# A hybrid decoder layer on one core: attention's products with the values, 40 places later in the scheduler's order of preference

## Chip, cores and metric

The kernel runs on one core of a Trainium2 chip. The metric is the device time of one execution in microseconds, and the number compared is the median of several executions. The kernel is written against a tile framework: the code names the work and the tiles, and a scheduler decides, before anything runs, in which fixed order each engine gets its instructions. On the chip every engine takes its own list in that order and waits on semaphores.

## What is computed

One decoder layer for a sequence of 2048 tokens, width 1024, in float32. The input is scaled and shifted by a conditioning vector; one projection feeds two groups of heads; their outputs are normalised, projected and added; a gated feed-forward network follows. The part that the change touches is group A, stick-breaking attention with 8 heads of 64:

```
z = einsum('bhqd,bhkd->bhqk', q, k) * scale
log_beta = log_sigmoid(z);  log_one_minus = where(causal, log_sigmoid(-z), 0)
tail = cumsum(log_one_minus, axis=3, reverse=True) - log_one_minus
w = where(causal, exp(log_beta + tail), 0)
out = einsum('bhqk,bhkd->bhqd', w, v)
```

Each weight is a sigmoid times the product of (1 - sigmoid) over all keys between it and the query, so a running product goes backwards over the keys. The last line is the product with the values.

## The kernel before

The sequence is cut into four tiles of 512 tokens (`t` = 0 to 3). `attend(t)` works through 8 heads; for each head it goes backwards over the key tiles `jt` = t to 0. One pair (head, key tile) is a step, so there are 8 x (1 + 2 + 3 + 4) = 80 steps. A step has two halves.

- **Four rows of 128 queries.** For each: two matmuls into the PSUM tile `z` (L549, L550), two sigmoids on ScalarE into `pp` and `beta` (L551, L552), on the diagonal two masks on GpSimd (L554, L556), the backward running product on VectorE (L563) and the multiplication of `beta` with it (L565; GpSimd for two rows of the four, VectorE for the others).
- **Four blocks of 128 keys** (`kb`). For each: up to four transposes of the weights on TensorE into the PSUM tile `wt` (L573), a copy `wh` on ScalarE that rounds to the matmul's format (L577), the remainder `wl = wt - wh` on VectorE (L578), and the products with the values, one with `wh` (L579) and one with `wl` (L581), both accumulated in the PSUM tile `o_ps`.

There are two buffers each of `wt`, `wh` and `wl`, and one of `o_ps`. So the transposes of block 2 wait until `wh` and `wl` of block 0 have been read out of `wt`. When a head is done, `o_ps` is copied and added into `ot` (L585, L586) and stored; the next head's first product waits for that.

Between the steps stands other work, "side work" below: `spread` takes from two generators in turn, so that the code order is a mixture. Beside `attend(t)` run the gated linear attention of tile t, the projections of tile t+1 (L293 to L295: 24 matmuls for one column tile; L302 to L304) and the preparation of later weights. Beside the last three heads of the last tile runs the mixer's output stage (L758, L791, L443 and the lines about them); lines L919 to L936 set it up, and stand in the code behind five heads of the last tile.

The scheduler numbers every instruction in the order of the code. Going through a simulated time, it gives each engine, of the instructions whose inputs and buffers it holds for ready, the one with the smallest number. `Urgent(engine, n)` shifts that number by n for the calls that go through it (a negative n makes it larger, so the instruction is less preferred). Before the change `act`, `dve` and `pool` have a positive shift, and `lazy`, with -90, is used for the mixer's output projection. The products of attention have their plain number through `pe`.

Of the kernel before, what the change touches and what calls it, by code (L numbers as in the profile page):

```python
# [60 lines left out]
NS3 = 21  # L61
NS0 = 35
LAZY = 90
PLO = (0,2)
ORD = 1
WP = 5.1
# [20 lines left out]
def layer(tc, x, c, w_ada, b_ada, w_in, gla_w_gate, gla_b_gate, sb_norm_g, gla_norm_g, w_out,  # L87
          ln1_g, ln1_b, w_ff_gate, w_ff_up, conv_w, conv_b, w_down, ln2_g, ln2_b, out):
    nc = tc.nc
# [15 lines left out]
    act, dve, pool = Urgent(nc.scalar), Urgent(nc.vector), Urgent(nc.gpsimd)  # L105
    pe = nc.tensor
    lazy = Urgent(nc.tensor, -LAZY) if LAZY else nc.tensor
    x, out = x[0], out[0]
    w_ada, w_in, w_out = w_ada[0], w_in[0], w_out[0]
    w_ff_gate, w_ff_up, w_down = w_ff_gate[0], w_ff_up[0], w_down[0]  # L110
# [100 lines left out]
    with tc.tile_pool(name="ada", bufs=1, reuse_waits="tile") as ada:  # L211
# [36 lines left out]
        for n in FIRST:  # L248
            ada_cols(KT + done, n, wa_first if done == 0 else None)
            ada_cols(done, n)  # L250
            cs = slice(done * P, (done + n) * P)
# [274 lines left out]
    def attend(t):  # L526
        for h in range(8):
            p, half = h // 2, h % 2
            rs = slice(64 * half, 64 * half + 64)
            q2 = sb.tile([P, 2, TQ], F32R, name="q2")  # L530
            for j in range(2):
                for rep in range(2):
                    nc.sync.dma_start(q2[64 * rep:64 * rep + 64, j, :].bitcast(F32), dq[p][t][j, rs, :])
            o_ps = psm.tile([P, TQ], F32, name="o_ps", bufs=1)
            carry = [None] * NB
            for jt in range(t, -1, -1):
                k2 = sb.tile([P, TQ], F32R, name="k2", bufs=3)
                for j in range(2):
                    nc.sync.dma_start(k2[64 * j:64 * j + 64, :].bitcast(F32), dk[p][jt][j, rs, :])
                v2 = sb.tile([P, NB, P], F32R, name="v2", bufs=3)  # L540
                nc.sync.dma_start(v2.bitcast(F32), dv[h // 4][jt][:, :, h % 4, :])
                ws = []
                for i in range(NB):
                    n = P * (i + 1) if jt == t else TQ
                    beta = sb.tile([P, TQ], F32, name="beta", bufs=NBETA)
                    pp = sb.tile([P, TQ + 1], F32, name="pp", bufs=NPP)
                    z = psm.tile([P, TQ], F32, name="z")
                    qs = slice(i * P, (i + 1) * P)
                    pe.matmul(z[:, 0:n], q2[:, 0, qs], k2[:, 0:n], start=True, stop=False)  # L549
                    pe.matmul(z[:, 0:n], q2[:, 1, qs], k2[:, 0:n], start=False, stop=True)  # L550
                    nc.scalar.activation(pp[:, 0:n], z[:, 0:n], AF.Sigmoid, scale=-1.0)  # L551
                    nc.scalar.activation(beta[:, 0:n], z[:, 0:n], AF.Sigmoid)  # L552
                    if jt == t:
                        nc.gpsimd.affine_select(pp[:, n - P:n], pp[:, n - P:n], pattern=[[-1, P]],  # L554
                                                compare_op=ALU.is_gt, fill=1.0, base=0, channel_multiplier=1)
                        nc.gpsimd.affine_select(beta[:, n - P:n], beta[:, n - P:n], pattern=[[-1, P]],  # L556
                                                compare_op=ALU.is_gt, fill=0.0, base=0, channel_multiplier=1)
                        nc.gpsimd.memset(pp[:, n:n + 1], 1.0)
                        first = 1.0
                    else:  # L560
                        first = carry[i][:, 0:1]
                        nc.gpsimd.tensor_copy(pp[:, TQ:TQ + 1], first)
                    nc.vector.tensor_tensor_scan(pp[:, 0:n][:, ::-1], pp[:, 0:n][:, ::-1],  # L563
                                                 beta[:, 0:n], first, ALU.mult, ALU.bypass)
                    (nc.gpsimd if i in PMU and jt < PMJ else nc.vector).tensor_mul(beta[:, 0:n], beta[:, 0:n], pp[:, 1:n + 1])  # L565
                    carry[i] = pp
                    ws.append(beta)
                for kb in range(NB):
                    q0 = kb if jt == t else 0
                    ks = slice(kb * P, (kb + 1) * P)  # L570
                    wt = psm.tile([P, TQ], F32, name="wt")
                    for i in range(q0, NB):
                        pe.transpose(wt[:, i * P:(i + 1) * P], ws[i][:, ks], ident)  # L573
                    wh = sb.tile([P, TQ], F32R, name="wh")
                    wl = sb.tile([P, TQ], F32R, name="wl")
                    cs = slice(q0 * P, TQ)
                    nc.scalar.copy(wh[:, cs], wt[:, cs])  # L577
                    nc.vector.tensor_sub(wl[:, cs], wt[:, cs], wh[:, cs])  # L578
                    pe.matmul(o_ps[:, cs], v2[:, kb, :], wh[:, cs],  # L579
                                     start=(jt == t and kb == 0), stop=False)  # L580
                    pe.matmul(o_ps[:, cs], v2[:, kb, :], wl[:, cs],  # L581
                                     start=False, stop=(jt == 0 and kb == NB - 1))
                yield WU if jt < t else WD
            ot = sb.tile([64, TQ], F32, name="ot", bufs=1)
            nc.scalar.copy(ot, o_ps[64:P, :])  # L585
            nc.vector.tensor_add(ot, ot, o_ps[0:64, :])  # L586
            nc.sync.dma_start(do[p][t][rs, :], ot)
            yield 0.0
# [190 lines left out]
    def mixer_out(t, ahead=None, n_ahead=1):  # L779
# [7 lines left out]
        for i in range(8):  # L787
# [13 lines left out]
            act.copy(hi, o)  # L801
            (nc.gpsimd if i in PLO else dve).tensor_sub(lo, o, hi)
            oh.append(hi)
# [95 lines left out]
    for t in range(NT - 1):  # L899
        spread(attend(t), 8 * (t + 2), 8 * (WD + t * WU), with_ada(between(t), ada_todo), S0 * (WP * 25 + WC * 8 + WL))  # L900
    last = attend(NT - 1)
    spread(last, LASTN * (NT + 1), LASTN * (WD + (NT - 1) * WU), with_ada(between(NT - 1), ada_todo), S3 * (WP * 13 + WC * 8))
    for f in ada_todo:
# [460 lines left out]
```

## Time and profile before

| | us |
|---|---|
| median of 3 runs | 2909.52 (2899.4 to 2913.5) |
| the profiled execution, its time | 2910.72 |
| the profiled execution, its span | 2909.0 |
| TensorE busy in the span | 2695.8 (93%) |
| VectorE busy in the span | 2092.0 (72%) |
| mean granted TensorE clock | 0.955 of full speed |

The span is from the first to the last instruction; the profiled execution's time is 1.7 us longer. Attention runs from 108 to 1431 us of the span; after it comes the rest of the mixer and the feed-forward network. Busy time of a matmul contains its way through the array, so rows of busy matmuls overlap, and the distance between two starts is what a matmul costs the one behind it.

### The profile page before, as it was taken

The numbers are of one execution on the slowest core, as the hardware profiler recorded it, in microseconds if no ns is written. First come the engines' busy times: TensorE is split into PE (matmuls) and PEld (weight loads), VectorE is DVE, ScalarE is ACT, GpSimd is POOL, SyncE is SP. The second block draws the span as 40 slices with busy tenths as digits, with TensorE's granted clock in tenths as the row PEclk, the third lists the DMA queues.
The fourth block names the chain that finished last, engine by engine and source line by source line (L and its number), as shares of the span: only waits on it lengthen the run. The fifth ranks groups of instructions, "written<-read, shape, count | busy, mean of one in ns | idle before, by whom it ended". The sixth has DMA issues, their size and how long they took to land. (4 is left out here: it accounts for less than half of the span.)

```text
span 2909.0 us, 38667 instructions
## 1 busy us (share of the span) xinstructions
PE 2695.8 (93%) x13123; PEld 2176.0 (75%) x13123; DVE 2092.0 (72%) x2984; ACT 1126.2 (39%) x1955; POOL 1206.8 (41%) x1271
## 2 busy tenths in 40 slices
PE   7989998989999988989779999898999999999998
PEld 6867887777788765567558778786788888788886
DVE  6375568568878878897676867776777777255988
ACT  2443244365656546534322333223322324332331
POOL 2550222155457674454573455754655554100000
PEclk8989999999999999989789999999999999999999
DMA  8977865767589876466795365545633334655564
GB/s 315 362 251 259 273 237 187 249 193 248 185 261 312 295 245 196 140 200 198 272 335 178 114 182 170 176 133 157 182 110 113 105 106 151 194 169 157 175 211 130
DMA packets 438173, 591.04 MB, mean 203 GB/s; under 512 B 28926, under 2 KB 276952, under 8 KB 437976
## 3 DMA queue, kind: packets, MB, share of 16 engines
q1 hardware_dynamic: 436248, 582.28, 61.9%
q0 software_dynamic: 1728, 6.29, 0.6%
q8 instruction: 104, 1.70, 0.2%
q14 instruction: 93, 0.76, 0.1%
HBM read 417.14 MB, written 171.32 MB: 202 GB/s over the span
## 5 line engine op out<-in xcount | busy, mean ns | idle before, releaser
L563 DVE TENSOR_TENSOR_SCAN pp<-pp,beta 128x512 f32<-128x512 f32 (+2 forms) x320 | 401.5, 1269 | 70.5 <-POOL beta L556 41.7
L565 POOL TENSOR_TENSOR beta<-beta,pp 128x512 f32<-128x512 f32 (+2 forms) x160 | 205.3, 1283 | 291.2 <-DVE pp L563 248.7
L1043 PE MATMUL acc<-t,w_lo 128*128 128x512 f32 x640 | 248.0, 395 | 16.4 <-DVE w_lo L102 16.4
L1041 PE MATMUL acc<-t,w_hi 128*128 128x512 f32 x640 | 252.2, 395 | 4.8 <-ACT k L1099 2.5
L1042 PE MATMUL acc<-t,w_hi 128*128 128x512 f32 x640 | 251.2, 393 | 2.1 <-POOL t L102 2.1
L578 DVE TENSOR_TENSOR wl<-wt,wh 128x512 fp32r<-128x512 f32 (+1 forms) x320 | 185.5, 597 | 71.6 <-ACT wh L577 71.2
L577 ACT CAST wh<-wt 128x512 fp32r<-128x512 f32 (+1 forms) x320 | 161.8, 530 | 180.9 <-PE wt L573 172.9
L551 ACT ACTIVATE pp<-z 128x512 f32<-128x512 f32 (+2 forms) x320 | 173.3, 544 | 138.2 <-PE z L550 83.5
L102 POOL TENSOR_TENSOR w_lo<-wsum,w_hi 128x1024 fp32r<-128x1024 f32 x80 | 204.6, 2558 | 30.4 <-ACT w_hi L102 30.4
L102 ACT CAST w_hi<-w_raw 128x512 fp32r<-128x512 f32 (+2 forms) x169 | 121.4, 740 | 247.5 <-PE acc L1042 93.0
L293 PE MATMUL acc<-hh,w_hi 128*128 128x512 f32 x480 | 194.9, 407 | 3.6 <-DVE st L102 3.0
L573 PE MATMUL wt<-ident,beta 128*128 128x128 f32 x1088 | 184.2, 286 | 14.6 <-DVE beta L565 6.3
L294 PE MATMUL acc<-hl,w_hi 128*128 128x512 f32 x480 | 192.6, 402 | 1.4 <-DVE hl L102 1.4
L295 PE MATMUL acc<-hh,w_lo 128*128 128x512 f32 x480 | 191.4, 400 | 0.5 <-POOL w_lo L102 0.5
L552 ACT ACTIVATE beta<-z 128x512 f32<-128x512 f32 (+2 forms) x320 | 171.2, 543 | 22.6 <-PE wt L573 22.6
L581 PE MATMUL o_ps<-wl,v 128*128 128x512 f32 (+1 forms) x320 | 135.0, 426 | 44.9 <-DVE wl L578 42.5
L573 PEld LDWEIGHTS wt<-ident,beta 128*128 128x128 f32 x1088 | 139.9, 147 | 46.2 <-DVE beta L565 8.8
L1043 PEld LDWEIGHTS acc<-t,w_lo 128*128 128x128 f32 x640 | 121.4, 190 | 45.2 <-DVE w_lo L102 19.8
L549 PE MATMUL z<-k,q 128*128 128x512 f32 (+2 forms) x320 | 140.9, 444 | 13.2 <-ACT beta L552 10.7
L102 ACT CAST w_hi<-wsum 128x1024 fp32r<-128x1024 f32 x80 | 84.0, 1050 | 176.9 <-PE wt L1042 72.8
L102 DVE TENSOR_TENSOR wsum<-w_raw 128x512 f32<-128x512 f32 x80 | 102.8, 1288 | 66.5 <-POOL w_lo L102 54.2
L554 POOL TENSOR_SCALAR_AFFINE_SELECT pp<-pp 128x128 f32<-128x128 f32 x128 | 56.0, 438 | 226.7 <-ACT pp L551 223.1
(341 smaller groups left out, 7603.5 us busy)
## 6 DMA issues: line engine op xcount, KB each, us to landing
w_raw<-in_w_ff_gate_dram SPq DMA_DIRECT2D x48, 512.0 KB
w_raw<-in_w_ff_up_dram SPq DMA_DIRECT2D x48, 512.0 KB
k<-dk SPq DMA_DIRECT2D x160, 128.0 KB
v<-dv SPq DMA_DIRECT2D x80, 256.0 KB
da<-cv SPq DMA_DIRECT2D x40, 512.0 KB
dsa<-cv SPq DMA_DIRECT2D x80, 256.0 KB
w_hi<-dwi_0h SPq DMA_DIRECT2D x39, 512.0 KB
w_lo<-dwi_0l SPq DMA_DIRECT2D x39, 512.0 KB
```

The costliest lines, as they stand in the source:

```text
L102: return f(*args, **kw)
L293: nc.tensor.matmul(ps, hi[:, k % 4, cs], xh[k], start=(k == 0), stop=False)
L294: nc.tensor.matmul(ps, hi[:, k % 4, cs], xl[k], start=False, stop=False)
L295: nc.tensor.matmul(ps, lo[:, k % 4, cs], xh[k], start=False, stop=(k == nk - 1))
L551: nc.scalar.activation(pp[:, 0:n], z[:, 0:n], AF.Sigmoid, scale=-1.0)
L563: nc.vector.tensor_tensor_scan(pp[:, 0:n][:, ::-1], pp[:, 0:n][:, ::-1], beta[:, 0:n], first, ALU.mult, ALU.bypass)
L565: (nc.gpsimd if i in PMU and jt < PMJ else nc.vector).tensor_mul(beta[:, 0:n], beta[:, 0:n], pp[:, 1:n + 1])
L573: pe.transpose(wt[:, i * P:(i + 1) * P], ws[i][:, ks], ident)
L578: nc.vector.tensor_sub(wl[:, cs], wt[:, cs], wh[:, cs])
L1041: nc.tensor.matmul(ps, w[0][:, k, :], t[k][:, 0, :], start=first and k == 0, stop=False, **add)
L1042: nc.tensor.matmul(ps, w[0][:, k, :], t[k][:, 1, :], start=False, stop=False, **add)
L1043: nc.tensor.matmul(ps, w[1][:, k, :], t[k][:, 0, :], start=False, stop=k == 3, **add)
```

## The change

The products with the values are issued through a second wrapper, which makes their number larger by 40. Nothing is added or removed: the same instructions, tiles, buffers and DMAs. What may differ is the order in which the scheduler lays down the instructions of each engine, and, by its simulated time, the order on the other engines and queues.

```
+OLATE = 40
...
+    late = Urgent(nc.tensor, -OLATE)
...
-                    pe.matmul(o_ps[:, cs], v2[:, kb, :], wh[:, cs],
+                    late.matmul(o_ps[:, cs], v2[:, kb, :], wh[:, cs],
                                      start=(jt == t and kb == 0), stop=False)
-                    pe.matmul(o_ps[:, cs], v2[:, kb, :], wl[:, cs],
+                    late.matmul(o_ps[:, cs], v2[:, kb, :], wl[:, cs],
                                      start=False, stop=(jt == 0 and kb == NB - 1))
```

## Rows read from the trace of the kernel before

**Rows 1.** Stretches: length, busy us (instructions) of each engine, TensorE clock, DMA share, GB/s.
```profile
100.00:400.00 300.00, 280.11 (x1674) 240.16 (x1674) 177.64 (x302) 120.82 (x240) 89.72 (x173) 0.93 0.80 270
400.00:600.00 200.00, 184.94 (x1086) 151.85 (x1085) 133.46 (x222) 76.26 (x166) 49.46 (x103) 0.97 0.69 226
600.00:1000.00 400.00, 377.94 (x2223) 316.34 (x2222) 321.39 (x400) 240.82 (x464) 228.97 (x313) 0.98 0.74 247
1000.00:1100.00 100.00, 88.14 (x500) 65.67 (x501) 80.54 (x104) 49.21 (x100) 67.92 (x83) 0.93 0.78 259
1100.00:1435.00 335.00, 288.16 (x1221) 200.73 (x1222) 287.42 (x446) 157.28 (x311) 170.84 (x197) 0.88 0.60 190
1435.00:2909.00 1474.00, 1396.73 (x6041) 1133.74 (x6039) 1039.25 (x1424) 455.34 (x636) 568.41 (x380) 0.98 0.53 165
```

**Rows 2.** TensorE's waits, 100 to 1435 us: us in total, times, longest.
```profile
PE o_ps L581 <- DVE wl L578: 42.5, 38, 4.3
PE z L549 <- ACT beta L552: 10.7, 14, 2.1
PE o_ps L579 <- ACT wh L577: 6.6, 6, 4.1
...
PE o_ps L579 <- DVE ot L586: 3.6, 3, 1.8
...
PE wt L573 <- DVE wl L578: 2.2, 3, 1.5
...
PE o_ps L581 <- DVE rn_mv L410: 1.8, 1, 1.8
...
PE o_ps L579 <- ACT beta L552: 0.5, 1, 0.5
```

**Rows 3.** Timeline of TensorE, third tile of queries, 665 to 669 us.
```profile
665.27 0.39 PE L295 MATMUL acc<-hh,w_lo 128*128 128x512 f32 x1
665.49 0.39 PE L579 MATMUL o_ps<-wh,v 128*128 128x512 f32 x1
665.72 0.39 PE L293 MATMUL acc<-hh,w_hi 128*128 128x512 f32 x1
...
666.63 0.39 PE L581 MATMUL o_ps<-wl,v 128*128 128x512 f32 x1
666.85 0.39 PE L579 MATMUL o_ps<-wh,v 128*128 128x512 f32 x1
667.09 0.38 PE L573 MATMUL wt<-ident,beta 128*128 128x128 f32 x2
667.22 0.48 PE L581 MATMUL o_ps<-wl,v 128*128 128x512 f32 x1
667.54 0.82 PE L573 MATMUL wt<-ident,beta 128*128 128x128 f32 x6
668.11 0.48 PE L294 MATMUL acc<-hl,w_hi 128*128 128x512 f32 x1
```

**Rows 4.** Timeline of all engines, last tile of queries, 1104 to 1114 us.
```profile
1104.11 0.39 PE L579 MATMUL o_ps<-wh,v 128*128 128x512 f32 x1
1104.12 1.88 DVE L563 TENSOR_TENSOR_SCAN pp<-pp,beta 128x512 f32<-128x512 f32 x1 [0.37 <-POOL beta L556]
...
1105.92 1.26 DVE L578 TENSOR_TENSOR wl<-wt,wh 128x512 fp32r<-128x512 f32 x2
1106.63 0.19 PEld L581 LDWEIGHTS o_ps<-wl,v 128*128 128x128 f32 x1 [2.53 <-DVE wl L578]
1106.64 0.50 PE L581 MATMUL o_ps<-wl,v 128*128 128x512 f32 x1 [2.14 <-DVE wl L578]
...
1106.97 0.40 PE L579 MATMUL o_ps<-wh,v 128*128 128x512 f32 x1
...
1107.21 0.60 PE L573 MATMUL wt<-ident,beta 128*128 128x128 f32 x4
...
1107.56 0.48 PE L581 MATMUL o_ps<-wl,v 128*128 128x512 f32 x1
...
1113.30 0.80 PE L581 MATMUL o_ps<-wl,v 128*128 128x512 f32 x1 [1.16 <-DVE wl L578]
```

**Rows 5.** Who waits for the transposes, copies and last products, whole span.
```profile
ACT wh L577 <- PE wt L573: 172.9, 108, 7.0
...
DVE wl L578 <- ACT wh L577: 71.2, 44, 7.4
...
ACT ot L585 <- PE o_ps L581: 55.1, 14, 15.6
```

**Rows 6.** Ends of heads 16, 24, 27, 29, 30, 31 and 32, and set-up of the mixer (timelines).
```profile
646.08 0.58 ACT L585 COPY ot<-o_ps 64x512 f32<-64x512 f32 x1
...
960.05 0.58 ACT L585 COPY ot<-o_ps 64x512 f32<-64x512 f32 x1
...
1114.13 0.58 ACT L585 COPY ot<-o_ps 64x512 f32<-64x512 f32 x1 [0.52 <-PE o_ps L581]
...
1115.82 0.84 PE L931 MATMUL acc<-ident,o_st 128*48 128x128 f32 x3
...
1209.72 0.58 ACT L585 COPY ot<-o_ps 64x512 f32<-64x512 f32 x1
...
1265.45 0.58 ACT L585 COPY ot<-o_ps 64x512 f32<-64x512 f32 x1 [5.64 <-PE o_ps L581]
...
1349.13 0.58 ACT L585 COPY ot<-o_ps 64x512 f32<-64x512 f32 x1 [5.06 <-PE o_ps L581]
...
1430.57 0.58 ACT L585 COPY ot<-o_ps 64x512 f32<-64x512 f32 x1 [6.14 <-PE o_ps L581]
```

**Rows 7.** One form each of the copy and the remainder: line, engine, busy us, mean ns.
```profile
L578 DVE TENSOR_TENSOR wl<-wt,wh 128x512 fp32r<-128x512 f32 x224 | 148.5, 677 | 64.1 <-ACT wh L577 64.0
...
L577 ACT CAST wh<-wt 128x512 fp32r<-128x512 f32 x224 | 128.3, 593 | 140.5 <-PE wt L573 137.7 <-DVE hh L102 1.9
```

## The prediction

> **What bounds the kernel now.** I read the stretches first, then who waits for whom on TensorE, then the order of its instructions in two timelines. The stretches [rows 1] show two regimes. After 1435 us the program is TensorE's, 1396.7 us of 1474.0, and no product with values is left there: that half can change only through what attention hands to it. In attention (100 to 1435 us) TensorE is idle for 19.9 + 15.1 + 22.1 + 11.9 + 46.8 = 115.8 us (length less busy time, row by row), and VectorE fills up: 59% of 100 to 400 us, 80% of 600 to 1000, 86% of 1100 to 1435. The granted clock is 0.88 in that last stretch; with two levels, 1.2 and 2.4 GHz, a mean of 0.88 is some 80 of 335 us at the lower one (0.12 x 2 x 335). So a gain has to come out of 115.8 us of idle time, or out of the clock that follows it.
>
> The waits [rows 2] put 42.5 + 6.6 + 3.6 + 1.8 + 0.5 = 55.0 us of this before products with values, almost all of it before the second one, which needs the remainder `wl` from VectorE. That is what invites moving the products back.
>
> The ends of the heads [rows 6] show that attention's chain lags behind the code. The set-up of the mixer (L931) stands in the code behind the fifth head of the last tile, head 29, and runs at 1115.8, just after head 27 has ended: 2 heads, 8 steps ahead. A step is 28 instructions for the rows (four times two matmuls, two sigmoids, one edge copy, the running product, the multiplication) and 32 for the blocks (four times four transposes, two copies, two products), so side work is some 480 numbers ahead. The timeline at 665 us [rows 3] looks the same: a product that comes ready is put between two matmuls of a column tile that are ready themselves; the products are already the most urgent ones there.
>
> **What 40 places reach.** A block is 8 instructions, so behind a product of block 0 stand 24 of the three later blocks and then at most 16 of whatever the code has next (fewer if requests for tiles are numbered too). Within a step, then, all later transposes now come before the earlier products, whenever both are ready. Against side work that is hundreds of numbers ahead, 40 changes nothing; against the next step's `z`, which ran long before, neither.
>
> When do both come ready? The transposes of block 2 wait for the buffer that `wl` of block 0 leaves; the second product of block 0 waits for the same `wl`. Today the order is [rows 4]: second product of block 0 at 1106.64, first of block 1 at 1106.97, the four transposes of block 2 at 1107.21. In [rows 3] it is 666.63, 666.85, 667.09. After the change the transposes go first. The same holds for block 3 behind block 1; blocks 0 and 1 of the next step lie over 40 away and keep their place. So two blocks in each of 80 steps: 160 blocks.
>
> **Cost of each part.**
> - *Transposes earlier.* Two products out of the way are 667.09 - 666.63 = 0.46 us at the full clock. Upper end: every block is waited for, 160 x 0.46 = 73.6 us. Lower end: nothing, if TensorE is full or VectorE is late anyway. What the end feels passes over ScalarE's copy to VectorE [rows 5]: ScalarE waited 108 times for transposes, but it has slack (38 to 60% busy in the stretches of attention [rows 1]); VectorE, the fuller one, waited 44 times for the copy, 71.2 us. If half of these are for blocks 2 and 3, 22 x 0.46 = 10.1 us; if all, 20.2 us. I take 10.
> - *Products later.* They go back by four transposes, 1107.56 - 1107.21 = 0.35 us. Who waits? The `wh` and `wl` buffers: `wl` of block 2 needs the one that the second product of block 0 reads. Cover: the copy of block 2 lies between, 593 ns of ScalarE [rows 7] against 0.46 us of products. So nothing; with the cover gone 160 x 0.35 = 56 us. The last two products of a head have no transposes behind them in their step, so `ot`, which waited 55.1 us for last products [rows 5], moves only where up to 16 of the next instructions pass them: 16 x 0.23 = 3.7 us at a head's end. I put 2 us on this in all; the upper end is below, as a rival.
> - *The 42.5 us before the second product.* At 1104.11 TensorE has issued the first product of block 0, and stands until 1106.64. Behind the waiting product are a product of block 1, and then transposes that need the very remainder waited for: `wl` is late because a running product of 1.88 us stands before it on VectorE [rows 4]. Putting the transposes in front leaves the stall and changes its name. Value 0; bound, 55.0 us gone.
> - The Trainium skill ("TensorE: Matmul & The Clock Gate", Part 2: What happens when you issue a matmul) says that matmuls stay in program order and that only weight loads are pulled ahead of running ones. By that rule a stall is only saved if something ready is laid before the waiting matmul, so a swap of two that wait for one remainder is worth 0 in place of the 10 us. The trace agrees that nothing overtakes, and not that the load is ahead: the load of the values starts at 1106.63 and its matmul at 1106.64.
> - *DMAs, other engines.* The same set. Their order is drawn anew by the scheduler's simulated time, which no row prices; 39 us a head between 646 and 960 us ((960.05 - 646.08) / 8) and 84 us for the one that ends at 1349 [rows 6] show how uneven the pace is. I leave its sign open and let it widen the range.
>
> Sum: -10 + 2 = -8 us on the execution's own 2910.7 gives 2902.7; that execution lies 1.2 us above the median, so 2901.5, rounded to **2902**.
>
> **The rivals.**
> 1. *The stalls do go.* If the scheduler's simulated time has `wl` ready much earlier than the chip has it, 40 places put side work of the last heads or of the first two tiles, where the code order is close, in front of the wait. Two thirds of 55.0 us are 37 us: 2873, and more if the clock of 0.88 rises. For it: 46.8 us idle and 84 and 81 us for the last two heads against 56 for head 30 [rows 6]. Against it: side work lies far ahead in most of attention.
> 2. *Nothing.* TensorE's list only swaps neighbours, VectorE stays as late as it was (86% busy in the last stretch): 2910, the change not doing what it says. For it: the stall at 1104 us.
> 3. *Slower: last products are passed by side work at a head's end.* `o_ps` has one buffer, so the copy into `ot`, then the next head's first product, wait; two blocks later the copy buffers are full. Price 3.7 us a head's end; with 7 of 32 such places 26 us, less the 2 already counted: 2934. It decides from 4 heads on (4 x 3.7 = 14.8 us). For it: the last three heads already wait 5.6, 5.1 and 6.1 us for the last product before `ot` [rows 6]. Against it: side work is ahead, and there is `z` work of the next head in between.
>
> **How the numbers follow.** 0.5%, about what a measurement here can tell from no change, is 14.5 us: faster is below 2895, slower above 2924. The forecast has a chance of 0.40, with a range of its own of 2888 to 2914, and 0.10 of it lies below 2895. Rival 1 has 0.24 (all faster), rival 2 0.15 (all within), rival 3 0.21 (all slower). So faster 0.10 + 0.24 = 0.34, same 0.30 + 0.15 = 0.45, slower 0.21. The range runs from 2866, which leaves out some 0.10 of rival 1, to 2936, which leaves out 0.08 of rival 3.
>
> **What the next profile would show.** Right: in a step, four transposes stand between the remainder of block 0 and its second product; the wait of L581 for `wl` falls from 42.5 us, and that of L573 for `wl`, 2.2 us now, takes most of it; VectorE's 71.2 us for the copy fall by some 10; head ends in the third tile, 646 to 960 us, come a few us closer. Rival 1: TensorE's idle time in attention falls well below 115.8 us, and the clock of the last stretch is above 0.88. Rival 3: `ot` waits more than 55.1 us, and the last heads take longer than 84 and 81 us. Wrong altogether if the difference lies after 1435 us, or if the order on TensorE differs by more than such swaps.

## The result, and the profile after

The changed kernel is slower: 2929.42 us (median of 7 runs, 2922.02 to 2937.97) against 2911.97 us (7 runs, 2899.40 to 2914.16). The ratio is 1.0065, 95% interval 1.0050 to 1.0080. That is 17.5 us, more than the 0.5% that the prediction set for a difference; it lies inside the range of 2866 to 2936 and on the other side of the forecast of 2902.

The profiled execution of the changed kernel took 2922.02 us (span 2920.3) and was the fastest of its seven, so the trace shows 11.3 us of the 17.5. It also had the highest mean granted clock of the seven, 0.960 against 0.952 to 0.957 in the others and 0.955 in the profiled execution before; what the others lose beyond this trace was not traced. Code lines stand two further down: transposes L575, copy L579, remainder L580, `z` L551 and L552, running product L565, `ot` L587. The products have the helper's line L103 now, because they go through the wrapper.

The stretches, answering to [rows 1]; the last row is a stretch that reaches past attention:

```profile
100.00:400.00 300.00, 278.75 (x1706) 237.46 (x1705) 181.74 (x307) 122.96 (x244) 90.20 (x173) 0.97 0.83 277
400.00:600.00 200.00, 186.01 (x1102) 153.60 (x1101) 136.69 (x224) 80.15 (x173) 56.34 (x115) 0.96 0.66 219
600.00:1000.00 400.00, 366.41 (x2155) 307.96 (x2154) 323.62 (x394) 238.84 (x456) 216.96 (x308) 0.97 0.74 242
1000.00:1100.00 100.00, 88.52 (x472) 66.75 (x471) 89.99 (x109) 52.77 (x105) 67.07 (x86) 0.91 0.77 250
1100.00:1435.00 335.00, 287.00 (x1240) 200.68 (x1240) 279.44 (x437) 154.45 (x302) 172.99 (x189) 0.89 0.60 193
1435.00:2909.00 1474.00, 1400.32 (x6060) 1136.65 (x6058) 1032.89 (x1407) 456.22 (x637) 566.66 (x380) 0.98 0.53 165
...
100.00:1640.00 1540.00, 1379.32 (x7385) 1097.55 (x7384) 1141.99 (x1691) 703.57 (x1361) 694.62 (x932) 0.94 0.71 235
```

The same long stretch of the kernel before:

```profile
100.00:1640.00 1540.00, 1400.26 (x7444) 1113.16 (x7444) 1141.64 (x1705) 702.14 (x1362) 703.36 (x934) 0.94 0.71 236
```

TensorE's idle time, length less busy time, rose from 115.8 us in attention [rows 1] to 21.25 + 13.99 + 33.59 + 11.48 + 48.00 = 128.3 us. From 100 to 1640 us it rose from 139.7 to 160.7. The mean clock of that stretch is 0.94 in both, so in this execution the clock isn't where the time went. The first part of the page gives the balance over the whole span:

```profile
PE 2688.2 (92%) x13123; PEld 2172.9 (74%) x13123; DVE 2104.4 (72%) x2984; ACT 1131.8 (39%) x1957; POOL 1201.3 (41%) x1271
```

TensorE is busy for 2688.2 us, 7.6 less than the 2695.8 before (the same instructions, at a mean clock of 0.960 against 0.955), and idle for 2920.3 - 2688.2 = 232.1, where it was 213.2: 18.9 more, less 7.6, is the span's 11.3. A marker behind attention shows when the loss is complete: the first matmul of the feed-forward network, before (the upper fence) and after (source view: count, shortest/median/longest ns, first and last start):

```profile
L1041 PE MATMUL acc<-t,w_hi x640: 387/389/632, 1594.1 to 2473.1; 128*128 128x512 f32 x160
```

```profile
L1043 PE MATMUL acc<-t,w_hi x640: 388/390/629, 1606.0 to 2484.4; 128*128 128x512 f32 x160
```

It starts 11.9 us later, and its last one 11.3 us later: all that this execution lost was lost before 1606 us.

TensorE's waits of 100 to 1435 us, answering to [rows 2]:

```profile
PE wt L575 <- DVE wl L580: 33.4, 25, 3.6
PE z L551 <- ACT beta L554: 14.2, 15, 2.0
PE o_ps L103 <- DVE wl L580: 14.1, 13, 2.3
PE wt L575 <- DVE beta L567: 12.6, 6, 3.9
PE o_ps L103 <- ACT wh L579: 8.5, 7, 4.1
```

The stall on the remainder has changed its name. Products waited 42.5 us for `wl` and transposes 2.2; now products wait 14.1 and transposes 33.4. The sum was 44.7 and is 47.5. The wait of transposes for weights from VectorE has doubled, to 12.6 us; its row before:

```profile
PE wt L573 <- DVE beta L565: 6.3, 5, 2.2
```

Who waits for the transposes, copies and products over the whole span, answering to [rows 5]:

```profile
ACT wh L579 <- PE wt L575: 166.1, 103, 7.3
...
ACT ot L587 <- PE o_ps L103: 62.5, 15, 15.7
...
DVE wl L580 <- ACT wh L579: 47.0, 33, 5.4
...
ACT wh L579 <- PE o_ps L103: 26.9, 22, 6.1
...
DVE wl L580 <- PE o_ps L103: 10.6, 6, 5.2
```

VectorE waits 24.2 us less for the copy (71.2 before). The last two rows are the price: copies that wait for products to free their buffer went from 4.4 us (the row below, of before) to 26.9, and remainders that do, from no such row to 10.6.

```profile
ACT wh L577 <- PE o_ps L579: 4.4, 5, 1.5
```

A place in the timeline of TensorE (start, length, engine, line, operation; what it waited for):

```profile
995.93 0.40 PE L296 MATMUL acc<-hl,w_hi 128*128 128x512 f32 x1
999.48 1.97 PE L575 MATMUL wt<-ident,beta 128*128 128x128 f32 x8 [3.16 <-DVE wl L580]
1001.11 0.78 PE L103 MATMUL o_ps<-wl,v 128*128 128x512 f32 x1
1001.68 0.63 PE L103 MATMUL o_ps<-wh,v 128*128 128x512 f32 x1
1002.11 0.63 PE L103 MATMUL o_ps<-wl,v 128*128 128x512 f32 x1
1002.53 0.63 PE L551 MATMUL z<-k,q 128*128 128x512 f32 x1
1002.96 0.63 PE L552 MATMUL z<-k,q 128*128 128x512 f32 x1
1003.39 0.63 PE L297 MATMUL acc<-hh,w_lo 128*128 128x512 f32 x1
```

Eight transposes, of two blocks, stand in a row at 999.48, and three products come behind them. Two of these need the very remainders that the transposes wait for; only the one with a copy (1001.68) can have been ready before. TensorE stands 3.16 us, while a half-done column tile (L296, then L297 at 1003.39) lies behind in its list. With the products in front TensorE would have waited here for the same remainder, so the place doesn't show a stall that the new order made.

The ends of heads 24, 29, 30, 31 and 32, answering to [rows 6]:

```profile
947.97 0.58 ACT L587 COPY ot<-o_ps 64x512 f32<-64x512 f32 x1
...
1189.84 0.58 ACT L587 COPY ot<-o_ps 64x512 f32<-64x512 f32 x1
...
1265.43 0.58 ACT L587 COPY ot<-o_ps 64x512 f32<-64x512 f32 x1 [0.96 <-PE o_ps L103]
...
1356.71 0.58 ACT L587 COPY ot<-o_ps 64x512 f32<-64x512 f32 x1 [0.61 <-PE o_ps L103]
...
1441.22 0.58 ACT L587 COPY ot<-o_ps 64x512 f32<-64x512 f32 x1 [14.29 <-PE o_ps L103]
```

Head 24 ends 12.1 us earlier than before and head 29 19.9 us earlier. Then the lead goes: 0.0 at head 30, 7.6 us late at head 31, 10.7 at head 32. Cut at those ends, the stretches after are:

```profile
100.00:1190.42 1090.42, 995.23 (x5800) 816.44 (x5798) 816.17 (x1170) 555.08 (x1101) 477.79 (x748) 0.96 0.74 243
1190.42:1441.80 251.38, 218.26 (x901) 155.67 (x901) 197.47 (x304) 94.66 (x180) 125.77 (x121) 0.87 0.59 194
1441.80:1640.00 198.20, 165.84 (x687) 125.44 (x686) 128.35 (x219) 53.83 (x82) 91.05 (x64) 0.93 0.70 246
```

and before, in the same way:

```profile
100.00:1210.30 1110.30, 1021.61 (x5853) 829.70 (x5853) 814.98 (x1183) 558.80 (x1112) 494.56 (x754) 0.95 0.74 243
1210.30:1431.15 220.85, 193.83 (x828) 141.86 (x828) 183.49 (x287) 85.58 (x167) 112.34 (x115) 0.87 0.62 201
1431.15:1640.00 208.85, 184.82 (x766) 141.60 (x765) 143.17 (x236) 57.75 (x84) 96.45 (x66) 0.93 0.69 239
```

Up to head 29 TensorE did 26.4 us less work in 19.9 us less time, so it idled 6.5 us more (95.2 against 88.7). In the last three heads TensorE is busy 24.4 us longer, about what was put off, and idle 6.1 us longer: 30.5 us together. From head 32 to 1640 us idle time rises by another 8.3, and 6.3 of this is one wait, before transposes of `xc` (L842, two further down after the change), which prepare the input of the feed-forward network. TensorE's waits of 1450 to 1480 us before, then of 1450 to 1490 after:

```profile
PE acc L842 <- DVE rn_mv L379: 2.0, 1, 2.0
```

```profile
PE acc L844 <- DVE rn_ra L384: 8.3, 1, 8.3
```

The earlier heads were bought with side work put off, not with idle time filled.

How far the order changed was counted over TensorE's list of 12,655 matmuls and transposes, as the scheduler laid it down. In all 160 blocks (2 and 3 of 80 steps) the transposes now stand ahead of the second product of two blocks earlier; in the kernel before they did in 13. In 22 of the 80 steps all transposes of block 3 stand even ahead of the second product of block 0 (before: none), as at 999.48; 14 of these steps have eight transposes in blocks 2 and 3, the other 8, on the diagonal, three. But of all pairs of instructions less than 120 places apart in the new list, 35,316 have changed sides, and the predicted swap can make only 960 of them: two products with each of 480 transposes (four in a block, two and one in blocks 2 and 3 on the diagonal). 294 of the 960 stood that way before. Some 29,000 are attention's work now ahead of side work: 13,755 pairs with transposes, 7,435 with `z`, about 7,850 with products.

### The profile page after: what moved, and what is told of

Read it like the earlier page. It is cut to its first block, busy times and chain, and to the rows that moved or that the text cites. A ratio compares the mean times of both kernels' runs of the same rounds, so it can differ in the third digit from the quotient of the medians.

```text
span 2920.3 us, 38789 instructions
## 1 busy us (share of the span) xinstructions
PE 2688.2 (92%) x13123; PEld 2172.9 (74%) x13123; DVE 2104.4 (72%) x2984; ACT 1131.8 (39%) x1957; POOL 1201.3 (41%) x1271
## 5 line engine op out<-in xcount | busy, mean ns | idle before, releaser
L565 DVE TENSOR_TENSOR_SCAN pp<-pp,beta 128x512 f32<-128x512 f32 (+2 forms) x320 | 408.4, 1290 | 62.4 <-POOL beta L558 33.9
L567 POOL TENSOR_TENSOR beta<-beta,pp 128x512 f32<-128x512 f32 (+2 forms) x160 | 198.1, 1238 | 265.4 <-DVE pp L565 229.7
L575 PE MATMUL wt<-ident,beta 128*128 128x128 f32 x1088 | 191.3, 293 | 56.0 <-DVE wl L580 33.4
L579 ACT CAST wh<-wt 128x512 fp32r<-128x512 f32 (+1 forms) x320 | 163.7, 528 | 197.2 <-PE wt L575 166.1
L580 DVE TENSOR_TENSOR wl<-wt,wh 128x512 fp32r<-128x512 f32 (+1 forms) x320 | 185.8, 597 | 59.5 <-ACT wh L579 47.0
L103 ACT CAST w_hi<-w_raw 128x512 fp32r<-128x512 f32 (+2 forms) x169 | 121.3, 740 | 252.6 <-PE acc L1044 90.7
L103 POOL TENSOR_TENSOR w_lo<-wsum,w_hi 128x1024 fp32r<-128x1024 f32 x80 | 203.9, 2548 | 31.8 <-ACT w_hi L103 31.7
L575 PEld LDWEIGHTS wt<-ident,beta 128*128 128x128 f32 x1088 | 138.3, 149 | 98.0 <-DVE wl L580 44.2
L297 PE MATMUL acc<-hh,w_lo 128*128 128x512 f32 x480 | 191.7, 400 | 0.7 <-POOL w_lo L103 0.7
L296 PE MATMUL acc<-hl,w_hi 128*128 128x512 f32 x480 | 190.6, 398 | 0.0
L554 ACT ACTIVATE beta<-z 128x512 f32<-128x512 f32 (+2 forms) x320 | 171.8, 543 | 12.8 <-PE wt L575 12.7
L103 PE MATMUL o_ps<-wl,v 128*128 128x512 f32 (+1 forms) x320 | 138.1, 435 | 17.5 <-DVE wl L580 14.1
L103 DVE TENSOR_TENSOR w_lo<-w_raw,w_hi 128x512 fp32r<-128x512 f32 (+1 forms) x136 | 131.7, 992 | 30.3 <-ACT w_hi L103 30.3
L103 ACT CAST w_hi<-wsum 128x1024 fp32r<-128x1024 f32 x80 | 84.0, 1050 | 177.4 <-PE wt L1044 78.1
L103 DVE TENSOR_TENSOR wsum<-w_raw 128x512 f32<-128x512 f32 x80 | 102.5, 1283 | 68.0 <-POOL w_lo L103 53.9
L567 DVE TENSOR_TENSOR beta<-beta,pp 128x512 f32<-128x512 f32 (+1 forms) x160 | 147.8, 924 | 4.5 <-POOL pp L564 0.7
```

Source lines behind the costliest of these rows:

```text
L103: return f(*args, **kw)
L296: nc.tensor.matmul(ps, hi[:, k % 4, cs], xl[k], start=False, stop=False)
L297: nc.tensor.matmul(ps, lo[:, k % 4, cs], xh[k], start=False, stop=(k == nk - 1))
```

## The experiments

Five readings were put to the test.

- **Transposes first.** The new order in the 160 blocks costs the time: TensorE stands before transposes with ready products and side work behind.
- **Held-back products.** The larger number of the products costs it: buffers and last products come later.
- **One place.** The loss belongs to the first three tiles of queries or to the last, where side work runs out, or to the ends of heads (rival 3).
- **Attention pulled ahead.** Side work is put off, as the head ends show, and is missing as filling later.
- **A new draw.** The shift alters the scheduler's simulated times, all of its order is laid anew, and the time is one of the many that such orders give, whatever the shift was for.

All results, in the order of the runs. Ratios are to the kernel before in the same session (its median was 2910.6 to 2914.9 us). "Blocks" is the count just described, of 160; "standing" is the time in us that TensorE stood before attention's own matmuls (`z`, `wt`, `o_ps`), 100 to 1450 us, summed from the view of waits; "idle" is TensorE's idle time from 100 to 1640 us; "last three" is from the end of head 29 to the end of head 32; "`xc`" is the wait before the transposes of `xc` behind 1450 us. "Standing" and the columns right of it are from one profiled execution each.

| kernel | median us | ratio | 95% interval | blocks | standing | idle | last three | `xc` |
|---|---|---|---|---|---|---|---|---|
| before | 2911.97 | 1 | | 13 | 82.6 | 139.7 | 221 | 2.0 |
| after | 2929.42 | 1.0065 | 1.0050-1.0080 | 160 | 101.8 | 160.7 | 251 | 8.3 |
| e1_first3 | 2915.57 | 1.0005 | 0.9990-1.0020 | 102 | 90.7 | 143.8 | 230 | 0.0 |
| e2_last1 | 2921.21 | 1.0033 | 1.0020-1.0046 | 71 | 91.8 | 145.8 | 238 | 0.6 |
| e3_instep | 2941.90 | 1.0110 | 1.0092-1.0128 | 160 | 106.6 | 159.3 | 258 | 6.8 |
| e4_beyond | 2924.44 | 1.0048 | 1.0030-1.0066 | 14 | 95.1 | 147.5 | 231 | 9.1 |
| e5_one | 2934.95 | 1.0078 | 1.0060-1.0095 | 11 | 96.8 | 161.0 | 243 | 8.2 |
| e6_twelve | 2933.59 | 1.0075 | 1.0057-1.0092 | 160 | 99.8 | 164.1 | 254 | 0.4 |
| e7_only_second | 2920.78 | 1.0031 | 1.0019-1.0042 | 160 | 103.0 | 152.8 | 244 | 2.5 |
| e8_only_first | 2913.38 | 1.0006 | 0.9992-1.0020 | 38 | 93.4 | 146.0 | 228 | 0.9 |
| e9_z_one | 2906.36 | 0.9983 | 0.9970-0.9995 | 13 | 83.8 | 143.2 | 214 | 1.8 |
| e10_sigmoid_one | 2914.74 | 1.0011 | 1.0001-1.0021 | 13 | 91.8 | 145.9 | 224 | 2.0 |
| e11_q_load | 2913.03 | 1.0011 | 1.0001-1.0021 | 15 | 85.0 | 142.0 | 215 | 2.6 |
| e12_eighty | 2938.97 | 1.0088 | 1.0066-1.0110 | 160 | 95.5 | 160.0 | 257 | 8.9 |
| e13_wt_earlier | 2924.54 | 1.0050 | 1.0031-1.0069 | 160 | 95.2 | 152.6 | 254 | 6.8 |
| e14_both_later | 2915.31 | 1.0016 | 0.9997-1.0034 | 12 | 92.3 | 146.4 | 227 | 2.3 |
| e15_wt_later | 2933.27 | 1.0083 | 1.0053-1.0113 | 12 | 97.4 | 158.4 | 237 | 8.3 |
| e16_wt_150_later | 2915.56 | 1.0007 | 0.9989-1.0025 | 14 | 85.4 | 140.3 | 225 | 0.0 |
| e17_thirtysix | 2938.33 | 1.0085 | 1.0069-1.0101 | 160 | 101.6 | 155.5 | 261 | 8.7 |
| e18_forty_z_one | 2931.13 | 1.0062 | 1.0047-1.0077 | 160 | 101.6 | 156.6 | 254 | 4.2 |

### Where: the tiles, and the two parts of the shift

**e1_first3**: late in the first three tiles of queries alone (both product lines; edits are against the changed kernel where they show `late`).

```
-                    late.matmul(o_ps[:, cs], ...
+                    (late if t < NT - 1 else pe).matmul(o_ps[:, cs], ...
```

> Products 40 later in the first three query tiles only, plain number in the last tile. Theory A, the loss comes from the last tile, where the mixer's output stage stands beside the heads (the last head ended 10.7 us later, the 24th 12.1 us earlier): time within 5 us of the kernel before, 2907 to 2917 us, with heads up to the 24th some 12 us earlier. Theory B, the loss comes from the first three tiles, where TensorE did 11.5 us less work between 600 and 1000 us: 2924 to 2934 us. Theory C, no place causes it, each new draw of the order lands somewhere within about 0.7 percent either way: any value from 2892 to 2932, not additive with the run on the last tile alone.

**e2_last1**: late in the last tile alone.

```
-                    late.matmul(o_ps[:, cs], ...
+                    (late if t == NT - 1 else pe).matmul(o_ps[:, cs], ...
```

> Products 40 later in the last query tile only. Theory A: 2924 to 2934 us, the last head ending 10 to 15 us later. Theory B: 2907 to 2917 us. Theory C: any value from 2892 to 2932, and the sum of this difference and that of the first three tiles is not the whole.

1.0005 and 1.0033. The two halves give 0.4% together where the whole gives 0.65%, so the loss isn't the sum of two places. The last tile alone gives half of it.

**e3_instep**: each block's products so late that they come behind the rest of their own step and no further.

```
-    late = Urgent(nc.tensor, -OLATE)
+    late = [Urgent(nc.tensor, -o) for o in (30, 19, 8, 0)]
...
+                    late[kb].matmul(o_ps[:, cs], ...
```

> Products of the four blocks of a step 30, 19, 8 and 0 later: later transposes of the same step still come first, but no product reaches past its step. If the transposes coming first cost the time (products hold their copy buffers longer, new wait of the remainder for the products, 9.4 us): 2924 to 2934 us. If the reach past the step costs it: 2900 to 2917 us. Theory C: anywhere from 2892 to 2932.

**e4_beyond**: only the last block's products late, which is all that can be passed by work behind the step.

```
+                    (late if kb == NB - 1 else pe).matmul(o_ps[:, cs], ...
```

> Only the products of a step's last block 40 later, so no transposes of the step are put in front, only what the code has next. If the reach past the step costs the time (rival 3 of the prediction: the end of a head waits): 2924 to 2934 us, with more waiting before the copy of the finished head than 55.1 us. If the transposes cost it: 2907 to 2917 us. Theory C: anywhere from 2892 to 2932.

e3 gives 1.0110 with shifts too small for a product to be passed by code behind its step: the reach past the step isn't needed for a loss, here a larger one than the change's. Its stretch (100 to 1640 us) is idle as long as the changed kernel's, 159.3 us, and gets fewer instructions done in the same busy time at a clock of 0.93; over its span (2944.8 us) TensorE is idle 23.0 us longer than before and busy 12.8 us longer:

```profile
100.00:1640.00 1540.00, 1380.66 (x7329) 1098.40 (x7328) 1126.72 (x1670) 700.44 (x1354) 685.23 (x926) 0.93 0.71 234
```

```profile
PE 2708.6 (92%) x13123; PEld 2186.3 (74%) x13123; DVE 2103.5 (71%) x2984; ACT 1133.0 (38%) x1958; POOL 1197.4 (41%) x1271
```

e4 loses too, 1.0048, with the transposes in 14 blocks only. But `ot` waits 52.8 us for last products there, less than the 55.1 before [rows 5], so it isn't by the mechanism of rival 3. Its loss was unexplained at this point, and was what brought up the draw.

### How far: one place, twelve, and one product of two

**e5_one** and **e6_twelve**:

```
-OLATE = 40
+OLATE = 1
```

> All products 1 later instead of 40. Nothing of the change's own effect is left: transposes of the block after next stand in front of the second product in 11 of the 320 blocks (13 before the change, 165 after it); what remains is that the order is drawn again. Theory D, the transposes in front hold the copy buffers longer and this costs the time: within 5 us of the kernel before, 2907 to 2917 us. Theory C, a new draw of the order costs by itself (the kernel before is a good draw): 2918 to 2940 us; or a gain as large, if draws fall on both sides.

```
-OLATE = 40
+OLATE = 12
```

> All products 12 later: 160 blocks have the transposes of the block after next in front, as with 40, and no product reaches past the next block's transposes. Theory D: as slow as the change, 2922 to 2942 us. Theory C: anywhere from 2897 to 2942, with no relation to the 160.

One place costs 1.0078, as much as 40, with the transposes ahead of second products in 11 blocks, like before. Its premise was not met in full: the first product of the next block now stands behind the first of those transposes in all 160 blocks (before: 99), but behind all of them in only 98 (before: 95). It is nearly a draw alone. Twelve places give the transposes first in all blocks and 1.0075. The stretch of e5:

```profile
100.00:1640.00 1540.00, 1379.04 (x7369) 1095.68 (x7367) 1133.09 (x1685) 700.88 (x1355) 699.42 (x929) 0.94 0.71 235
```

**e7_only_second** leaves the product with `wh` at its plain number, **e8_only_first** the one with `wl`.

```
-                    late.matmul(o_ps[:, cs], v2[:, kb, :], wh[:, cs],
+                    pe.matmul(o_ps[:, cs], v2[:, kb, :], wh[:, cs],
```

> Only the product with the remainder wl 40 later (163 blocks with transposes in front of it). Theory D: as slow as the change, 2922 to 2942 us, and VectorE waits for products (9.4 us with the change from 600 to 800 us, no such wait in the largest rows before). Theory C: anywhere from 2897 to 2942.

```
-                    late.matmul(o_ps[:, cs], v2[:, kb, :], wl[:, cs],
+                    pe.matmul(o_ps[:, cs], v2[:, kb, :], wl[:, cs],
```

> Only the product with the copy wh 40 later (38 blocks with transposes in front of the second product). Theory D: less than half of the loss, 2912 to 2921 us. Theory C: anywhere from 2897 to 2942.

1.0031 with 160 blocks and 1.0006 with 38. Of the two alone only the shift of the second product loses, half of what both lose together, and it is the one that puts the transposes in front.

### A shift that has nothing to do with the products

The next three take the kernel before and shift something else by one to three places: the `z` matmuls, the second sigmoid, the loads of the queries.

```
+    one = Urgent(nc.tensor, -1)
...
-                    pe.matmul(z[:, 0:n], q2[:, 0, qs], ...
+                    one.matmul(z[:, 0:n], q2[:, 0, qs], ...
```

> The kernel before, with the matmuls into z 1 later and the products at their plain number. Nothing of the products' order against transposes changes; TensorE's list differs in some 560 of 12655 places, all of them from about the last two heads on. Theory C2, the end of attention (last three heads, 221 us before, 228 to 258 us in the runs so far) is a good draw in the kernel before and any new draw of it costs: 2917 to 2935 us. Theory D2, only products held back cost: 2907 to 2917 us.

```
+    one = Urgent(nc.scalar, -1)
...
-                    nc.scalar.activation(beta[:, 0:n], z[:, 0:n], AF.Sigmoid)
+                    one.activation(beta[:, 0:n], z[:, 0:n], AF.Sigmoid)
```

> The kernel before, with the second sigmoid 1 later on ScalarE. TensorE's list differs in some 350 places, all from about the last head on. Theory C2: 2917 to 2935 us. Theory D2: 2907 to 2917 us.

```
+    one = Urgent(nc.sync, -3)
...
-                    nc.sync.dma_start(q2[64 * rep:64 * rep + 64, j, :].bitcast(F32), ...
+                    one.dma_start(q2[64 * rep:64 * rep + 64, j, :].bitcast(F32), ...
```

> The kernel before, with the loads of the queries 3 later on the load queue. TensorE's list differs in some 1350 places from the first tile on; products keep their order against transposes. Theory C2: 2917 to 2935 us. Theory D2: 2907 to 2917 us. A gain would say that the draws fall on both sides.

0.9983, 1.0011 and 1.0011, all below the 2917 us from which theory C2 had expected them: not every new draw costs. These re-lay less of TensorE's list: 3,262, 1,113 and 5,500 pairs, against 21,340 for e5 and 35,316 for the change. e9 is the fastest kernel of the study, faster than before by 0.17% with an interval that stays below 1; its stretch holds nearly the idle time of before, 143.2 us:

```profile
100.00:1640.00 1540.00, 1396.81 (x7476) 1109.48 (x7475) 1146.41 (x1709) 705.74 (x1366) 712.67 (x938) 0.95 0.71 237
```

**e12_eighty** and, later, **e17_thirtysix** are the change with another size.

```
-OLATE = 40
+OLATE = 80
```

> All products 80 later (201 blocks with transposes in front). Theory D (held copy buffers cost in proportion): slower than with 40, 2932 to 2955 us, and VectorE and ScalarE wait more for products than the 10.6 and 26.9 us with 40. Theory C: anywhere from 2897 to 2942 us.

```
-OLATE = 40
+OLATE = 36
```

> Products 36 later instead of 40: transposes first in all 160 blocks as with the change, TensorE's list differs from the change's in 975 of 12655 places. If the transposes coming first set the loss: 2924 to 2936 us, as with 40. If the draw sets it: outside of that, between 2908 and 2950 us.

1.0088 and 1.0085. Both keep the blocks and the sign. Four places less than 40 change the size by 0.2%, with intervals that overlap.

### The transposes shifted instead

**e13_wt_earlier**: the products keep their number, the transposes get a smaller one. If held-back products cost the time, this is harmless; if the order of the two does, it isn't.

```
+    tr = Urgent(nc.tensor, 40)
...
-                        pe.transpose(wt[:, i * P:(i + 1) * P], ws[i][:, ks], ident)
+                        tr.transpose(wt[:, i * P:(i + 1) * P], ws[i][:, ks], ident)
```

> The kernel before, with the transposes 40 earlier and the products at their plain number: in all 160 blocks the transposes come before the second product of the block two before, as with the change. Theory M: as slow as the change, 2922 to 2942 us, TensorE standing 95 to 110 us before attention's matmuls (100 to 1450 us; 82.6 before, 101.8 with the change). Theory D: 2907 to 2920 us, since no product got a later number. Theory C: anywhere from 2897 to 2942.

**e14_both_later**: both late, so that they stand to each other as before.

```
-                        pe.transpose(wt[:, i * P:(i + 1) * P], ws[i][:, ks], ident)
+                        late.transpose(wt[:, i * P:(i + 1) * P], ws[i][:, ks], ident)
```

> Products and transposes both 40 later: the second product comes before the transposes again (12 of 160 the other way, 13 before the change, 160 with it); the first product of the next block still comes behind the first of them (160, against 99 before). Theory M: less than half of the loss, 2908 to 2922 us, standing 83 to 97 us. Theory D: 2922 to 2942 us. Theory C: anywhere.

e13 loses, 1.0050, and its waits of 100 to 1450 us show the stall under the transposes' name as in the changed kernel:

```profile
PE wt L102 <- DVE wl L579: 32.9, 25, 3.1
...
PE o_ps L582 <- DVE wl L579: 10.0, 9, 2.1
```

e14 gives 1.0016, with an interval that holds 1. So the larger number of the products falls as the cause: they don't have it in e13, which loses, and have it in e14, which loses a quarter of the change's 0.65%, if anything. Products that stand behind the transposes still free their buffers later in e13, so this says nothing about the buffers. The copies and remainders that wait for products do: in all they wait 12.4 us in e6, which loses 0.75%, and 22.2 us in e8, which loses nothing clear of noise (37.5 with the change, 4.4 before). So the loss doesn't go with that waiting. Rows of e6, then of e8:

```profile
ACT wh L579 <- PE o_ps L103: 10.7, 18, 2.0
```

```profile
ACT wh L579 <- PE o_ps L103: 22.2, 9, 6.2
```

**e15_wt_later** and **e16_wt_150_later**: the opposite order, the transposes 40 and 150 places later with plain products.

```
+    tr = Urgent(nc.tensor, -40)
...
+                        tr.transpose(wt[:, i * P:(i + 1) * P], ws[i][:, ks], ident)
```

> The kernel before, with the transposes 40 later: products keep coming first, as before (12 of 160), and attention's work goes as often before side work as behind it. Theory M: 2902 to 2917 us, standing 75 to 92 us. Theory C: anywhere from 2897 to 2942.

```
+    tr = Urgent(nc.tensor, -150)
```

> The kernel before, with the transposes 150 later: side work goes before attention's transposes in many places, so attention is behind, the mirror image of the change. Theory M: TensorE stands less before attention's matmuls than the 82.6 us of before (55 to 80 us), heads end later, and the time is 2890 to 2912 us, unless the last heads now end too late for the mixer (then above 2917 us with less standing). Theory C: anywhere from 2897 to 2942 us with no relation to the standing.

e15 was expected at 2902 to 2917 us and took 2933.27, ratio 1.0083, with the transposes first in 12 blocks. Its pairs are balanced (transposes and side work changed sides 3,919 times one way and 3,785 the other), so attention wasn't pulled ahead either; both readings miss. The stall on the remainder has grown under the product's name, 60.1 us against 42.5 [rows 2] (its waits, 100 to 1450 us):

```profile
PE o_ps L582 <- DVE wl L579: 60.1, 37, 9.4
```

e16 is the mirror of the change: side work now ahead of transposes in 32,991 of 70,412 pairs. It was expected at 2890 to 2912 us with less standing than before (55 to 80 us), and misses both: 2915.56 us and 85.4. Its time is that of before, 1.0007, and so is its idle time, 140.3 us:

```profile
100.00:1640.00 1540.00, 1399.70 (x7425) 1114.89 (x7424) 1144.49 (x1699) 706.48 (x1363) 729.12 (x934) 0.93 0.71 236
```

while its last head ends at 1453.36 us, 22.8 us later than before [rows 6] (timeline of ScalarE):

```profile
1453.36 0.58 ACT L586 COPY ot<-o_ps 64x512 f32<-64x512 f32 x1 [5.35 <-PE o_ps L582]
```

So a later end of attention's chain costs nothing by itself where TensorE's idle time stays as it was.

**e18_forty_z_one**: the change together with the edit of the fastest kernel.

```
+    one = Urgent(nc.tensor, -1)
...
+                    one.matmul(z[:, 0:n], q2[:, 0, qs], ...
```

> The change, and the matmuls into z 1 later (which alone gave a ratio of 0.9983): transposes first in all 160 blocks, TensorE's list differs from the change's in 937 places, from the second tile's heads on. If the transposes coming first set the loss: 2924 to 2936 us. If the draw sets it: outside of that, between 2908 and 2950 us.

1.0062, where the change and the gain of e9 together would be 1.0048, just inside the interval: whether the gain adds is not shown. Laying the list anew doesn't bring the change back to the time of before.

A third buffer of `wh` and `wl`, which would take away the copies' and remainders' wait for products, wasn't tried.

### What follows from all of them

Of eight kernels with the transposes first in all 160 blocks, all eight are slower, 1.0031 to 1.0110, mean 1.0071. Of nine with 38 blocks or fewer (e4, e5, e8 to e11, e14 to e16), the ratios are 0.9983 to 1.0083, mean 1.0027; two of these nine lose as much as the change. Transposes first always came with a loss, then, but the loss doesn't need them. The eight are not eight independent trials: the lists of e17 and e18 differ from the changed kernel's in 975 and 937 of 12,655 places.

What most losing kernels share is where the time lies. Over the twenty kernels of the table, the ratio goes with the idle time before 1640 us (correlation 0.90) and with the standing before attention's matmuls (0.81). The first is partly arithmetic, for all issue the same 13,123 matmuls and transposes; that is its point: most of the loss is idle time of TensorE in and just behind attention. The rest goes with the clock. In e3, the slowest, a third is longer busy time (12.8 of the 35.8 us by which its span is longer), and the median granted clock of the executions of e3, e12 and e17 is 0.952 to 0.953, beside 0.959 to 0.960 for the kernel before in the same sessions. Whether the clock falls because TensorE idles more was not tested.

One place stands out. The wait before the transposes of `xc`, behind attention, is 4.2 to 9.1 us in nine kernels, and these have ratios of 1.0048 to 1.0110. It is at most 2.6 us in the other eleven, of which only e6 is above 1.0033. The three of the nine kernels without the new order that lose more than 0.2%, e4, e5 and e15, are the three with this wait (e5's row, 1400 to 1640 us):

```profile
PE acc L844 <- DMA xc<-dx: 8.2, 1, 8.2
```

Where the wait is long, kernels with the transposes first in all blocks lose hardly more than those without (mean 1.0077 of six, 1.0070 of three); where it is short, 1.0053 of two stands against 1.0006 of six. In e5 and e15 it makes 6 of the 19 to 21 us of added idle time, and the longer stall on the remainder (44.7 us before, 57.3 and 60.5) another 13 and 16. No run changes this wait alone, so it marks the slow kernels and isn't shown to be what makes them slow.

## Why the prediction was wrong

Two steps failed: the 10 us of gain for earlier transposes, and the premise that 40 places leave attention's place against side work as it was.

**Right: the order in the step.** It said two blocks in each of 80 steps, 160 blocks, would get their transposes in front. They did, in all 160.

**Right: the stall keeps its length and changes its name.** 44.7 us became 47.5, with the transposes' wait for `wl` at 33.4 and the products' at 14.1. Rival 1, the stalls gone, is refuted: idle time rose. The prediction's remark that a weight load isn't ahead of its matmul fits 1106.63 us, where the matmul waited; in the trace before, around 666 us, loads start some 0.23 us ahead of theirs (666.18 and 666.40).

**Right in direction, and worth nothing: "Transposes earlier".** VectorE's wait for the copy fell by 24.2 us, more than twice the 10 of the text (10.6 came back as remainders that wait for products), and the heads of the third tile did end earlier, head 24 by 12.1 us. The step that failed is the next one, which took an earlier chain for an earlier end. Up to head 29 the lead was 19.9 us, with 26.4 us of TensorE's work put off; the last three heads got that work back, and 30.5 us of length. e16 shows the reverse, the last head 22.8 us later and the time unchanged. The text had said itself that a gain must come out of 115.8 us of idle time or out of the clock, and then counted 10 us that come out of neither. The 0.46 us for a block was too much as well: it was read at two places, and in 95 of the 160 blocks the transposes already stood ahead of one of the two products.

**Wrong by its size: "Products later", 2 us.** The cover, a copy of 593 ns, was weighed for one block behind one swap. In 22 of 80 steps the transposes of two blocks stand in front, and those of the second wait for the next remainder, so the products behind wait with them, and the buffers with the products: remainders waiting for products 0 to 10.6 us, copies 4.4 to 26.9. That is 33.1 us of new waiting, against the named bound, "with the cover gone", of 56 us and a value of nothing. Little of this need reach the end: e6 and e8 show that the loss doesn't go with this waiting.

**Wrong: "Against side work that is hundreds of numbers ahead, 40 changes nothing".** True of the numbers, not of the list. Some 29,000 pairs of attention's and side work changed sides against at most 960 of the swap. The numbers decide only between what the simulated time holds for ready, and the swap alters those times for everything behind it. The text left the sign of this open; what it lacked was a size. The runs give it: shifts of one to three places elsewhere moved the time by -0.17% to +0.11%, e15, whose order in the blocks is that of before, by +0.83%. By the text's own condition ("if the order on TensorE differs by more than such swaps") it was wrong altogether.

**Rival 3, the right sign for another reason.** The last three heads did take longer, 251.4 us against 220.9, and `ot` waited 62.5 us instead of 55.1. But e4, which has only its mechanism, shows 52.8 us of that wait. Heads 30 and 31 wait 0.96 and 0.61 us for their last product; only head 32 shows it, 14.29 us.

**Still open** is how the 17.5 us divide between the transposes in front and the draw. The means differ by 0.44%, and each group scatters by about 0.3%; the second was chosen for what it tells, not at random, and the first has kernels whose lists are nearly the same. Open too is why the wait before `xc` is long in some lists and short in others. That the transposes in front cost something by themselves is likely from eight losses in eight, and e7 would bound it at 0.42%, the upper end of its interval, if its draw were neutral, which nothing shows.

## What to carry to other kernels

In a list that a scheduler lays down ahead of time, a shift of priority re-lays thousands of places, so price that draw (here from 0.17% faster to 0.8% slower with the intended order absent) before the mechanism, look for the one long wait that a new draw may bring far from the edit, and try a few neighbours of the shift before believing a gain or a loss of that size. Where engines take their lists in order, an instruction put in front of a stall takes the stall over if it waits for the same data. Here a chain that ended earlier was worth nothing, since the fullest engine idled no less for it.

## What was not expected of the hardware

After the stand of 3.16 us that ends at 999.48 us in the changed kernel the next matmuls start 0.57 and then 0.43 us apart (1001.11, 1001.68, 1002.11, 1002.53), where the column tile before it has 0.23 (995.70 to 995.93); from 1005.39 us on they are at 0.23 again. The granted clock is 1.00 up to 998 us, is 0.63 from 998.00 to 999.50, within the stand, and 0.50 behind it, the lower of the two levels (1.2 GHz):

```profile
999.50:1005.00 5.50, 5.50 (x17) 4.73 (x18) 5.17 (x7) 2.76 (x5) 1.10 (x5) 0.50 1.02 352
```

So some 5 us at half the clock came with a stand of 3. For all that, the mean granted clock from 100 to 1640 us is 0.94 in both kernels, with 21.0 us more idle time in the changed one.
